# Seven-product blocks of a decoder trunk: another order of the halves, results given out one per half, standard units placed by a count of VectorE's work

## The chip, the core and the metric

The kernel runs on one core of one Trainium2 chip. The metric is the device time of one execution in microseconds (us): 1917.76 us before, the median of three runs (1916.74 to 1919.27).

## The reference

Two layers of a decoder trunk over 256 tokens of width 2048, all in float32:

```python
for l in range(DEPTH):
    h = rms_norm(x, norm1_g[l])
    z = h @ w_in[l]
    ...
    x = x + mixed @ w_out[l]
    h2 = rms_norm(x, norm2_g[l])
    x = x + (jax.nn.silu(h2 @ w_gate[l]) * (h2 @ w_up[l])) @ w_down[l]
```

What is left out is a gated spatial unit and a sliding-window attention that make `mixed`. The change touches only the last line, the feed-forward stage: gate and up projections (2048 to 5632 columns each), SwiGLU, and the down projection back to 2048.

## The kernel before

**Float32 from two parts.** A weight tile of 128 x 1024 numbers is loaded into a buffer `raw` (eight of them). ScalarE casts it to a rounded high part `wh` (`split2`, L127; five buffers), VectorE subtracts that from `raw` and gives the low part `wl` (L128; four buffers). TensorE then makes three matmuls for each product, high by high, high by low, low by high (`mm3`, L163 to L165). So each tile costs ScalarE one cast and VectorE one subtraction, and neither can run further ahead of TensorE than there are buffers.

**Standard units.** `unit` uses one tile for both token blocks: twelve matmuls of 512 columns. The down projection and block 0 of gate and up are made of these, 104 a layer, in PSUM banks named `dacc`. The down projection adds onto the residual: ScalarE copies the residual into a bank (`seed`, L1211) and the sum back out (`out_of`, L1237).

**Seven-product blocks.** For the other ten blocks of 512 columns (`S_BLOCKS`), gate and up for both token blocks are taken as one 2 x 2 product of matrices in seven multiplications in place of eight. The class `Lean` holds one block. Its methods `one` to `seven` are the seven products, each in four pieces i = 0 to 3 along the inner dimension. A piece is called a half: half of a unit's matmuls, six, from one tile. This text writes 5.2 for piece 2 of product five. The operands on the weight side are:

- 1.i and 3.i load a tile with SyncE. After 1.i's split, GpSimd issues a DMA that adds another weight tile onto that buffer (`onto`, L456). 5.i splits the sum.
- In 5.i VectorE also forms t2 = that sum + the buffer of 3.i (L471, recorded as L453), and GpSimd then issues a DMA that adds onto the buffer of 3.i. 6.i splits t2, 7.i splits the buffer of 3.i.
- 2.i loads a tile, and VectorE adds it onto t2 (recorded as L453 too); 4.i splits that.

`tc.issue_after` keeps each of these sums behind the split before it.

The products collect in five PSUM banks: m0 for one and two, m4 for three, m1 for five, m3 for six (which begins as a copy of m0, L476), m2 for seven and four. Results come out in between: m0 + six is copied out of the bank (L491), c21 = m2 + that (VectorE, recorded as L453), c21 is copied back into the bank m2 by ScalarE (L495) so that 4.i can add onto it, then c12, c22 and c12 once more on VectorE. Before, these steps stand in the method `two`, behind 2.0, 2.1, 2.2 and 2.3. Then `gated` takes Silu on ScalarE (L1162) and a multiplication on VectorE (L1163), and the activation is transposed by TensorE into `ps_f` (L246), cast (L1141) and split (L1142) for the down projection.

**What sets the order.** `lean_run` sorts all halves of all ten blocks by a table: `LEAN[m][i]` is the place of half i of product m within its block, and block n starts 28 places after block n-1. `lean_run` is a generator. The loop at L1300 takes one step of it and then as many standard units as keep their count on a straight line: 5 at first, 16 left at the end, and `HALVES` = 300 steps in between (280 halves, and two empty steps per block, after 4.3 and after 6.3). Beneath this, a scheduler settles the final order on each engine, and pools give out buffers as they come free. Each engine takes its own instructions in order, GpSimd's and SyncE's DMA issues among them.

Of the kernel before, what the change touches and what calls it, by code (L numbers as in the profile page):

```python
# [12 lines left out]
F32 = mybir.dt.float32  # L13
# [3 lines left out]
ALU = mybir.AluOpType  # L17
# [3 lines left out]
P = 128  # L21
# [73 lines left out]
def trunk(ctx, tc, x, xt, w_in, w_q, w_out, w_oa, w_uh, w_gate, w_up, w_down, sgu_w, sgu_g, consts,  # L95
# [13 lines left out]
    def f(t):  # L109
        return t.bitcast(F32)  # L110
# [6 lines left out]
        return raw  # L117

    last_wl = [None]

    def split2(raw):
# [3 lines left out]
        for j in range(0, 2, step):  # L125
            src = raw[:, j : j + step, :]
            nc.scalar.copy(wh[:, j : j + step, :], src)  # L127
            last_wl[0] = nc.vector.tensor_tensor(  # L128
                wl[:, j : j + step, :], src, f(wh[:, j : j + step, :]), ALU.subtract
            )  # L130
        return wh, wl
# [5 lines left out]
    def later(delay, fn):  # L137
        pending.append((clock[0] + delay, next(serial), fn))
# [280 lines left out]
    class Lean:  # L419
        def __init__(self, src, pairs, ext, out, end=lambda sg: None):  # L420
            self.src, self.out, self.end = src, out, end
            self.bank, self.raw, self.t2, self.z = {}, {}, {}, {}

            def a_op(k, t):
                return lambda p, h: pairs[p][:, h, k, t * P : (t + 1) * P]

            def e_op(n):
                return lambda p, h: ext[p][:, h, n, :]

            self.home = {  # L430
                1: (0, a_op(0, 0)), 2: (0, a_op(1, 0)), 3: (4, e_op(3)), 4: (2, a_op(1, 1)),
                5: (1, e_op(1)), 6: (3, e_op(2)), 7: (2, e_op(0)),
            }

        def acc(self, m):
            if m not in self.bank:
                self.bank[m] = pa.tile([P, NB], F32, tag="acc", name=f"m{m}")
            return self.bank[m]

        def half(self, n, raw, i):  # L440
            m, op = self.home[n]
            wh, wl = split2(raw)
            first, last = n in (1, 3, 5, 7) and i == 0, i == 3
            for j in range(2):
                ah, al = (op(2 * i + j, h) for h in range(2))
                mm3(
                    self.acc(m), ah, al, wh[:, j, :], wl[:, j, :], first and j == 0,
                    last and j == 1, m in (0, 2, 3),
                )
            tick(0.5)  # L450

        def add(self, out, x, y):
            nc.vector.tensor_tensor(out, x, y, ALU.add)  # L453

        def onto(self, dst, i):
            anchor[0] = nc.gpsimd.dma_start(dst, self.src(0, 1, i), accum_op=ALU.add)  # L456
# [10 lines left out]
        def five(self, i):  # L467
            self.half(5, self.raw[1, i], i)
            self.t2[i] = ap.tile([P, 2, NB], F32, tag="spt", name="t2", bufs=4)
            with tc.issue_after(last_wl[0].ins):  # L470
                self.add(self.t2[i], self.raw[1, i], self.raw[3, i])  # L471
            self.onto(self.raw[3, i], i)

        def six(self, i):
# [7 lines left out]
        def two(self, i):  # L482
            b21 = raw_load(self.src(1, 0, i))
            self.half(2, b21, i)
            with tc.issue_after(last_wl[0].ins):
                self.add(self.t2[i], self.t2[i], b21)
            z, bank = self.z, self.bank
            if i == 0:
                for v in ("m0", "c12", "c21", "c22"):
                    z[v] = zp.tile([P, NB], F32, tag="z", name=v)  # L490
                nc.scalar.copy(z["m0"], bank[3])  # L491
            elif i == 1:
                self.add(z["c21"], bank[2], z["m0"])
            elif i == 2:
                nc.scalar.copy(bank[2], z["c21"])  # L495
                self.add(z["c12"], bank[1], z["m0"])
            else:
                self.add(z["c22"], bank[1], z["c21"])
                self.add(z["c12"], bank[4], z["c12"])

        def four(self, i):
            self.half(4, self.t2[i], i)
            z, bank = self.z, self.bank
            if i == 0:
                self.out(0, bank[0], z["m0"], z["c12"])
            elif i == 3:
                later(1, lambda: self.out(1, bank[2], z["c21"], z["c22"]))
                self.end([z["m0"], z["c21"]])

    def lean_run(blocks):  # L510
        steps = sorted(
            (28 * n + LEAN[m][i], n, m, i) for n in range(len(blocks)) for m in range(7) for i in range(4)
        )
        for _, n, m, i in steps:
            b = blocks[n]
            (b.one, b.two, b.three, b.four, b.five, b.six, b.seven)[m](i)
            yield
# [108 lines left out]
    for lay in range(L):  # L626
# [510 lines left out]
        def act_T(b, c, sg, pairs_f=pairs_f):  # L1137
            ps = pm.tile([P, 2, SEQ], F32, tag="sm", name="ps_f")
            transpose_pair([sg[t][:, 2 * c * P : (2 * c + 2) * P] for t in range(NTOK)], ps)
            pair = tp.tile([P, 2, 2, SEQ], F32R, tag="aT", name="aT")  # L1140
            nc.scalar.copy(pair[:, 0], ps)  # L1141
            nc.vector.tensor_tensor(pair[:, 1], ps, f(pair[:, 0]), ALU.subtract)  # L1142
            pairs_f.setdefault(b, []).append(pair)

# [15 lines left out]

        def gated(t, psum, sg, c, rstd2=rstd2, nrstd2=nrstd2):
            nc.scalar.activation(sg, psum, AF.Silu, scale=rstd2[t])  # L1162
            nc.vector.scalar_tensor_tensor(sg, c, nrstd2[t], sg, ALU.mult, ALU.mult)  # L1163

        def s_block(b, lay=lay, pairs2=pairs2, ext2=ext2, gated=gated, act_later=act_later):
# [22 lines left out]
        def gate_up(b, even=even, act_later=act_later, seeds=seeds, left=left):  # L1188
            acc = yield from even(b, w_gate)
            sg = []  # L1190
            for t in range(NTOK):
                s = zp.tile([P, NB], F32, tag="z", name="sg")
                nc.scalar.activation(s, acc[t], AF.Silu, scale=rstd2[t])
                sg.append(s)
            acc = yield from even(b, w_up)
            for t in range(NTOK):
                nc.vector.scalar_tensor_tensor(
                    sg[t], acc[t], rstd2[t], sg[t], ALU.mult, ALU.mult
                )
                later(1.5 + 0.5 * t, lambda t=t: left[0] < NFF or seeds[0](0, t))  # L1200
            act_later(b, sg)
# [95 lines left out]
        done = 0  # L1297
        while done < FF_FIRST and next(other):
            done += 1
        for k, _ in enumerate(s_stream()):  # L1300
            while done < FF_FIRST + (k + 1) * (STD_UNITS - TAIL - FF_FIRST) / HALVES and next(other, False):
                done += 1
        seven_done[0] = True
        if lay < L - 1:
# [103 lines left out]
```

## Time and profile before

| what | value |
|---|---|
| median of the runs (3) | 1917.76 us |
| the profiled execution | 1915.93 us |
| its span, first to last instruction | 1914.2 us |
| TensorE busy | 1892.9 us, 99% |
| VectorE busy | 1685.7 us, 88% |
| ScalarE busy | 1400.8 us, 73% |
| granted TensorE clock | 1.000 |

In the profile, PE is TensorE, PEld its weight loads (which run beside the matmuls), DVE is VectorE, ACT ScalarE, POOL GpSimd, SP SyncE. A row of a group names line, engine, operation, what is written and read, shapes and count, then the busy time and the mean of one in ns, then the idle time of the engine ahead of it and who ended it. In a timeline the idle time stands in brackets at the end of a row. A chain of waits is followed back from the last instruction: each row is a start, a length and what ran or was waited for. Most executions agree within 0.3%.

### The profile page before, as it was taken

Reading aid. Unit: us, or ns where it says so; the run is one execution under the profiler, and the core shown is the slowest. Engines: PE = TensorE matmul, PEld = TensorE weight load, DVE = VectorE, ACT = ScalarE, POOL = GpSimd, SP = SyncE. Lnnn points to the kernel's source line nnn. Section 1 sums busy time; section 2 is a strip of 40 time slices with the busy share of each in tenths; the row PEclk is TensorE's granted clock in tenths of the full one; section 3 lists DMA queues with packets and bytes.
Section 4 is the critical chain, followed back from the end, with each engine's and each line's share of the span. In section 5 each row is a group of like instructions: output and inputs, shape, how many; then the busy total and the mean of one; then the engine's idle time right before and its main releaser. Section 6 shows DMA issues by size and latency. Waiting matters only on the chain.

```text
span 1914.2 us, 25497 instructions
## 1 busy us (share of the span) xinstructions
PE 1892.9 (99%) x8624; PEld 1544.8 (81%) x8624; DVE 1685.7 (88%) x1834; ACT 1400.8 (73%) x1880; POOL 218.2 (11%) x224
## 2 busy tenths in 40 slices
PE   9999999999999999999999999999999999999999
PEld 7887788888878878788888778888888888787887
DVE  7988988999889988989898888989999898988993
ACT  8668776777767777777776886767877676776774
POOL 0231001110111001100002200011110111011100
PEclk9999999999999999999999999999999999999999
DMA  9973669888988889878568648699888888888873
GB/s 355 262 285 132 189 208 241 240 223 245 259 233 218 246 246 240 224 230 257 188 219 290 192 153 233 209 259 244 220 237 255 239 235 231 242 242 239 224 236 119
DMA packets 123394, 442.15 MB, mean 231 GB/s; under 512 B 13696, under 2 KB 14080, under 8 KB 123264
## 3 DMA queue, kind: packets, MB, share of 16 engines
q1 hardware_dynamic: 94320, 336.59, 49.9%
q0 software_dynamic: 28224, 102.77, 29.3%
q8 instruction: 67, 1.10, 0.2%
q10 hardware_dynamic: 720, 1.18, 0.2%
q14 instruction: 63, 0.52, 0.1%
HBM read 438.39 MB, written 2.10 MB: 230 GB/s over the span
## 4 chain that ended last, share of the span: by engine, by line
PE 89%; DVE 4%; ACT 2%; DMA 2%; issue 2%; POOL 0%; SPq 0%; DVEq 0%; POOLq 0%; ACTq 0%
PE m L164 14%; PE m L163 14%; PE m L165 14%; PE dacc L163 11%; PE dacc L164 11%; PE dacc L165 11%; PE acc L164 3%; PE acc L165 3%; PE acc L163 3%; DMA raw<-in_w_up_dram 2%; DVE wl L128 1%; PE l L163 1%; PE l L164 1%; PE l L165 1%; PE ps_f L246 1%
## 5 line engine op out<-in xcount | busy, mean ns | idle before, releaser
L127 ACT CAST wh<-raw 128x1024 fp32r<-128x1024 f32 (+1 forms) x794 | 823.0, 1051 | 344.2 <-PE dacc L165 169.5
L128 DVE TENSOR_TENSOR wl<-raw,wh 128x1024 fp32r<-128x1024 f32 (+1 forms) x794 | 951.4, 1217 | 133.3 <-ACT wh L127 45.9
L164 PE MATMUL m<-wl,ext 128*128 128x512 f32 x704 | 274.8, 390 | 3.0 <-DVE wl L128 3.0
L163 PE MATMUL m<-wh,ext 128*128 128x512 f32 x704 | 275.6, 392 | 0.0
L165 PE MATMUL m<-wh,ext 128*128 128x512 f32 x704 | 274.3, 390 | 0.0
L456 POOL DMA_DIRECT2D raw<-in_w_up_dram x160 | 138.6, 870 | 1059.9 <-DVE wl L128 490.6
L163 PE MATMUL dacc<-wh,aT 128*128 128x512 f32 x624 | 243.2, 392 | 0.0
L164 PE MATMUL dacc<-wl,aT 128*128 128x512 f32 x624 | 243.1, 390 | 0.0
L165 PE MATMUL dacc<-wh,aT 128*128 128x512 f32 x624 | 243.1, 390 | 0.0
L128 DVE TENSOR_TENSOR wl<-t,wh 128x1024 fp32r<-128x1024 f32 x176 | 212.9, 1218 | 22.5 <-ACT wh L127 11.3
L127 ACT CAST wh<-t 128x1024 fp32r<-128x1024 f32 x176 | 184.6, 1052 | 39.7 <-PE m L165 23.0
L163 PE MATMUL m<-wh,hT 128*128 128x512 f32 x528 | 206.0, 391 | 0.0
L165 PE MATMUL m<-wh,hT 128*128 128x512 f32 x528 | 205.6, 389 | 0.0
L164 PE MATMUL m<-wl,hT 128*128 128x512 f32 x528 | 205.5, 389 | 0.0
L164 PEld LDWEIGHTS m<-wl,ext 128*128 128x128 f32 x704 | 132.2, 188 | 32.3 <-DVE wl L128 5.4
L165 PEld LDWEIGHTS m<-wh,ext 128*128 128x128 f32 x704 | 132.2, 188 | 27.5
L163 PEld LDWEIGHTS m<-wh,ext 128*128 128x128 f32 x704 | 132.2, 188 | 27.0
L165 PEld LDWEIGHTS dacc<-wh,aT 128*128 128x128 f32 x624 | 117.2, 188 | 24.5
L164 PEld LDWEIGHTS dacc<-wl,aT 128*128 128x128 f32 x624 | 117.2, 188 | 24.3 <-DVE wl L128 0.2
L163 PEld LDWEIGHTS dacc<-wh,aT 128*128 128x128 f32 x624 | 117.2, 188 | 24.0
L164 PEld LDWEIGHTS m<-wl,hT 128*128 128x128 f32 x528 | 99.2, 188 | 20.7 <-DVE wl L128 0.3
L165 PEld LDWEIGHTS m<-wh,hT 128*128 128x128 f32 x528 | 99.1, 188 | 20.5
(218 smaller groups left out, 2823.2 us busy)
## 6 DMA issues: line engine op xcount, KB each, us to landing
raw<-in_w_gate_dram SPq DMA_DIRECT2D x176, 512.0 KB, 5.2
raw<-in_w_down_dram SPq DMA_DIRECT2D x176, 512.0 KB, 5.0
raw<-in_w_up_dram POOLq DMA_DIRECT2D x160, 512.0 KB, 8.3
raw<-in_w_up_dram SPq DMA_DIRECT2D x96, 512.0 KB, 5.1
raw<-in_w_in_dram SPq DMA_DIRECT2D x68, 512.0 KB, 6.6
raw<-in_w_out_dram SPq DMA_DIRECT2D x48, 512.0 KB, 4.4
raw<-in_w_q_dram SPq DMA_DIRECT2D x32, 512.0 KB, 5.9
raw<-in_w_oa_dram SPq DMA_DIRECT2D x16, 512.0 KB, 3.7
```

What stands on the lines that cost most here:

```text
L127: nc.scalar.copy(wh[:, j : j + step, :], src)
L128: last_wl[0] = nc.vector.tensor_tensor(wl[:, j : j + step, :], src, f(wh[:, j : j + step, :]), ALU.subtract)
L163: nc.tensor.matmul(acc, ah, wh, start=first, stop=False, skip_group_check=again)
L164: nc.tensor.matmul(acc, ah, wl, start=False, stop=False, skip_group_check=again)
L165: nc.tensor.matmul(acc, al, wh, start=False, stop=last, skip_group_check=again)
L246: nc.tensor.transpose(ps[:, j, t * P : (t + 1) * P], blocks[t][:, j * P : (j + 1) * P], ident)
L456: anchor[0] = nc.gpsimd.dma_start(dst, self.src(0, 1, i), accum_op=ALU.add)
```

## The change

There are three parts.

1. *The order of the halves.* `LEAN` gets other places, and a block's period is 56 places in place of 28. The two empty steps per block are gone, and `HALVES` is 280.
2. *The results.* They no longer stand in `two` and `four`, but in a list, each with the product that must be finished for it. After each half, `settle` takes at most one from the list of each open block. Ahead of 4.0 it takes as many as are needed for the bank m2.
3. *The units.* `vec` counts VectorE's work in the order of the program: 1 for a split or a sum of a tile, 0.55 or 0.6 for the smaller ones. The loop compares this count with a usual course (1.47 per half and 1.02 per unit) and moves the count of units that are due by 0.4 of the difference. This begins after 28 steps and fades out over the last 28.

```diff
-HALVES = 30 * len(S_BLOCKS)
+HALVES = 28 * len(S_BLOCKS)
+HALF_LOAD = 1.47
+UNIT_LOAD = 1.02
+EVEN = 0.4
...
 LEAN = (
-    (0, 4, 8, 12), (24, 26, 27, 29), (6, 10, 14, 18), (30, 31, 33, 37), (7, 11, 15, 19),
-    (16, 20, 22, 23), (13, 17, 21, 25),
+    (0, 9, 17, 25), (48, 52, 55, 58), (10, 18, 26, 34), (58, 60, 64, 72), (14, 22, 30, 39),
+    (28, 36, 41, 42), (28, 36, 44, 57),
 )
...
+            self.results = [
+                ({6}, self.unite), ({7}, lambda: self.add("c21", 2, "m0")),
+                (set(), lambda: nc.scalar.copy(self.bank[2], self.z["c21"])),
+                ({5}, lambda: self.add("c12", 1, "m0")), (set(), lambda: self.add("c22", 1, "c21")),
+                ({3}, lambda: self.add("c12", 4, "c12")),
+                ({2}, lambda: self.out(0, self.bank[0], self.z["m0"], self.z["c12"])),
+                ({4}, self.finish),
+            ]
...
+        def settle(self, upto=None):
+            while self.results and self.results[0][0] <= self.done:
+                self.results.pop(0)[1]()
+                if upto is None or len(self.results) <= upto:
+                    break
...
         def half(self, n, raw, i):
             m, op = self.home[n]
+            if n == 4 and i == 0:
+                self.settle(5)
...
-            (28 * n + LEAN[m][i], n, m, i) for n in range(len(blocks)) for m in range(7) for i in range(4)
+            (56 * n + LEAN[m][i], n, m, i) for n in range(len(blocks)) for m in range(7) for i in range(4)
         )
...
-            if m in (3, 5) and i == 3:
-                yield
...
+            if k == 27:
+                load[0] = usual(k)
+
+            def due():
+                ahead = load[0] - usual(k)
+                more = EVEN * ahead * min(1, (HALVES - 1 - k) / 28) if k > 27 else 0
+                return min(FF_FIRST + (k + 1) * slope + more, STD_UNITS - TAIL)
```

**VectorE, from 5.0 to 7.0 of block 7, layer 0.** Before; t2 is the sum in 5.0, raw_6008 the buffer of 3.0, which is split at the end for 7.0; the splits between are 1.2, 4.3 of the block before (t2_5756), 3.1, 5.1 and 1.3:

```order
L453 TENSOR_TENSOR t2_6050<-raw_5916,raw_6008 128x1024
L128 TENSOR_TENSOR wl_6056<-raw_6053,wh_6055 128x1024
L128 TENSOR_TENSOR wl_6067<-t2_5756,wh_6066 128x1024
L128 TENSOR_TENSOR wl_6079<-raw_6076,wh_6078 128x1024
L128 TENSOR_TENSOR wl_6089<-raw_5985,wh_6088 128x1024
L453 TENSOR_TENSOR t2_6103<-raw_5985,raw_6076 128x1024
L128 TENSOR_TENSOR wl_6109<-raw_6106,wh_6108 128x1024
L128 TENSOR_TENSOR wl_6123<-raw_6008,wh_6122 128x1024
```

The same place on VectorE after the change, from the split of 1.2 on (the sum t2_6032 of 5.0 and the split of 4.3 stand right ahead of it); raw_6058 and raw_6138 are standard units, wl_6171 is 6.0, the last row is 7.0:

```order
L137 TENSOR_TENSOR wl_6048<-raw_6045,wh_6047 128x1024
L137 TENSOR_TENSOR wl_6061<-raw_6058,wh_6060 128x1024
L137 TENSOR_TENSOR wl_6081<-raw_6078,wh_6080 128x1024
L137 TENSOR_TENSOR wl_6099<-raw_5995,wh_6098 128x1024
L1191 SCALAR_TENSOR_TENSOR c21_5791<-c22_5792,nr_2723,c21_5791 128x512
L511 TENSOR_TENSOR t2_6108<-raw_5995,raw_6078 128x1024
L137 TENSOR_TENSOR wl_6114<-raw_6111,wh_6113 128x1024
L137 TENSOR_TENSOR wl_6141<-raw_6138,wh_6140 128x1024
L137 TENSOR_TENSOR wl_6159<-raw_6156,wh_6158 128x1024
L1169 TENSOR_TENSOR aT_6095<-ps_f_6090,aT_6095 128x512
L137 TENSOR_TENSOR wl_6171<-t2_6032,wh_6170 128x1024
L137 TENSOR_TENSOR wl_6181<-raw_6008,wh_6180 128x1024
```

Between the sum and the split of 7.0 stood five splits and one sum; now there are nine splits (two of them units), one sum and two smaller steps.

**ScalarE, the copy of c21 into the bank m2, block 6, layer 0.** Before; the casts are a unit, 1.0 of the next block, 2.3 and 4.0 (t2_5516), then the copy, then 4.1 (t2_5616):

```order
L127 CAST wh_5900<-raw_5898 128x1024
L127 CAST wh_5918<-raw_5916 128x1024
L127 CAST wh_5932<-raw_5930 128x1024
L127 CAST wh_5945<-t2_5516 128x1024
L495 COPY m2_5636<-c21_5856 128x512
L127 CAST wh_5957<-t2_5616 128x1024
```

The same place on ScalarE after the change; the casts are 2.3, (a copy of the residual into a bank,) 4.0, a unit, 4.1, 4.2 and a second unit:

```order
L136 CAST wh_5912<-raw_5910 128x1024
L1240 COPY dacc1_5879<-xres_111 128x512
L136 CAST wh_5925<-t2_5516 128x1024
L136 CAST wh_5938<-raw_5936 128x1024
L136 CAST wh_5954<-t2_5592 128x1024
L136 CAST wh_5965<-t2_5685 128x1024
L136 CAST wh_5979<-raw_5977 128x1024
L447 COPY m2_5668<-c21_5791 128x512
```

The copy stood right behind the cast of 4.0; now the casts of 4.1, 4.2 and two units are ahead of it.

**TensorE, the start of 4.0 at the same place.** Before, 4.0 follows 2.3 (m0):

```order
L164 MATMUL m0_5388<-wl_5933,hT_2806 128x512
L165 MATMUL m0_5388<-wh_5932,hT_2806 128x512
L163 MATMUL m2_5636<-wh_5945,hT_2359 128x512
L164 MATMUL m2_5636<-wl_5946,hT_2359 128x512
L165 MATMUL m2_5636<-wh_5945,hT_2359 128x512
```

After the change, a standard unit (dacc) stands between 2.3 and 4.0, and 4.0 begins ahead of that unit's last four matmuls:

```order
L172 MATMUL dacc0_5876<-wh_5938,aT_4592 128x512
L173 MATMUL dacc0_5876<-wl_5939,aT_4592 128x512
L172 MATMUL m2_5668<-wh_5925,hT_2359 128x512
L173 MATMUL m2_5668<-wl_5926,hT_2359 128x512
L174 MATMUL m2_5668<-wh_5925,hT_2359 128x512
L172 MATMUL m2_5668<-wh_5925,hT_2393 128x512
L173 MATMUL m2_5668<-wl_5926,hT_2393 128x512
L174 MATMUL m2_5668<-wh_5925,hT_2393 128x512
L174 MATMUL dacc0_5876<-wh_5938,aT_4592 128x512
```

Between the last matmul of 7.3, which c21 needs, and the first of 4.0 stood 2.1, 2.2, a unit, 1.0 of the next block and 2.3, 36 matmuls; now there are 2.3 and eight matmuls of the unit, 14.

More of the change, by code (lines that the diff above doesn't have):

```diff
@@ L438, in acc, with unite, add, finish @@
             return self.bank[m]
+        def unite(self):
+            for v in ("m0", "c12", "c21", "c22"):
+                self.z[v] = zp.tile([P, NB], F32, tag="z", name=v)
+            nc.scalar.copy(self.z["m0"], self.bank[3])
+        def add(self, out, bank, z):
+            vec(0.55)
+            nc.vector.tensor_tensor(self.z[out], self.bank[bank], self.z[z], ALU.add)
+        def finish(self):
+            later(1, lambda: self.out(1, self.bank[2], self.z["c21"], self.z["c22"]))
+            self.end([self.z["m0"], self.z["c21"]])
+        def settle(self, upto=None):
[3 more added lines that the diff above has]
+                    break
         def half(self, n, raw, i):
             m, op = self.home[n]
+            if n == 4 and i == 0:
+                self.settle(5)
             wh, wl = split2(raw)
@@ L449, in half @@
                 )
+            if last:
+                self.done.add(n)
             tick(0.5)
-        def add(self, out, x, y):
-            nc.vector.tensor_tensor(out, x, y, ALU.add)
         def onto(self, dst, i):
@@ L485, in two @@
             with tc.issue_after(last_wl[0].ins):
[L486 to L499, printed above, removed]
+                vec(1)
+                nc.vector.tensor_tensor(self.t2[i], self.t2[i], b21, ALU.add)
         def four(self, i):
             self.half(4, self.t2[i], i)
[L503 to L508, printed above, removed]
     def lean_run(blocks):
         steps = sorted(
-            (28 * n + LEAN[m][i], n, m, i) for n in range(len(blocks)) for m in range(7) for i in range(4)
+            (56 * n + LEAN[m][i], n, m, i) for n in range(len(blocks)) for m in range(7) for i in range(4)
         )
+        open_blocks = []
         for _, n, m, i in steps:
             b = blocks[n]
+            if m == 0 and i == 0:
+                open_blocks.append(b)
             (b.one, b.two, b.three, b.four, b.five, b.six, b.seven)[m](i)
+            for o in open_blocks:
+                o.settle()
+            open_blocks = [o for o in open_blocks if o.results]
             yield
-            if m in (3, 5) and i == 3:
-                yield
     def seven_low(src, pairs, ext, done, tag="hT"):
@@ L1299, in trunk, with usual @@
             done += 1
-        for k, _ in enumerate(s_stream()):
-            while done < FF_FIRST + (k + 1) * (STD_UNITS - TAIL - FF_FIRST) / HALVES and next(other, False):
+        load[0] = 0.0
+        begun = done
+        slope = (STD_UNITS - TAIL - FF_FIRST) / HALVES
+        def usual(k):
+            halves, units = k + 1, done - begun
+            return halves * HALF_LOAD + units * UNIT_LOAD
+        for k, _ in enumerate(s_stream()):
+            if k == 27:
[4 more added lines that the diff above has]
+                return min(FF_FIRST + (k + 1) * slope + more, STD_UNITS - TAIL)
+            while done < due() and next(other, False):
                 done += 1
```

12 lines of the change are left out of this document (11 added, 1 removed).

## The prediction

> **What bounds the kernel now.** I read the page first, then the waits, then the feed-forward stage in equal stretches, then the chain of waits inside one bad stretch. The engine line of the page, and one row of the waits:
>
> ```profile
> PE 1892.9 (99%) x8624; PEld 1544.8 (81%) x8624; DVE 1685.7 (88%) x1834; ACT 1400.8 (73%) x1880; POOL 218.2 (11%) x224
> ```
> ```profile
> ACT wh L127 <- DMA raw<-in_w_up_dram: 37.0, 27, 3.5
> ```
>
> TensorE has work for 99% of the span, so no reordering can win more than its gaps. The second row names something that recurs: ScalarE waits 27 times for an accumulating DMA. Now one clean stretch of the feed-forward stage, and the six with TensorE gaps (three in each layer; the columns are length, busy time of each engine with its instructions, clock, DMA share, GB/s):
>
> ```profile
> 345.00:440.00 95.00, 95.00 (x432) 78.60 (x431) 88.89 (x85) 72.28 (x87) 12.13 (x14) 1.00 0.88 239
> 535.00:630.00 95.00, 93.23 (x419) 76.83 (x418) 84.90 (x80) 68.48 (x78) 12.10 (x14) 1.00 0.87 234
> 630.00:725.00 95.00, 93.53 (x415) 76.63 (x415) 84.81 (x81) 67.89 (x77) 8.66 (x10) 1.00 0.85 237
> 725.00:820.00 95.00, 92.99 (x417) 76.22 (x416) 83.90 (x79) 67.28 (x78) 12.13 (x14) 1.00 0.88 242
> 1485.00:1580.00 95.00, 93.99 (x423) 77.53 (x422) 85.69 (x81) 69.66 (x79) 12.12 (x14) 1.00 0.87 236
> 1580.00:1675.00 95.00, 93.39 (x414) 76.39 (x413) 84.61 (x80) 66.91 (x77) 8.66 (x10) 1.00 0.84 236
> 1675.00:1770.00 95.00, 93.02 (x417) 76.17 (x415) 83.77 (x79) 68.02 (x78) 12.12 (x14) 1.00 0.87 241
> ```
>
> The gaps are 1.77 + 1.47 + 2.01 = 5.25 us in the first layer and 1.01 + 1.61 + 1.98 = 4.60 in the second: **9.85 us in all**, and nothing in this stage beside them. The clock is full everywhere. VectorE is busy 84 to 86 of 95 us where TensorE waits and 88.9 where it doesn't: it isn't short of time on average, it is late at moments. The chain of waits in the second stretch shows which:
>
> ```profile
> 667.08 1.15 DVE t L453
> 668.26 0.48 issue
> 668.75 7.84 DMA raw<-in_w_up_dram
> 676.68 1.06 ACT wh L127
> 677.77 1.14 DVE wl L128
> ...
> 684.09 0.49 ACT aT L1141
> 684.60 0.70 DVE aT L1142
> 685.35 0.65 PE ps_f L246 x4
> ```
>
> This is half 5.0 of block 7: VectorE's sum t2, then GpSimd's accumulating DMA into the same buffer, then ScalarE's cast of that buffer for half 7.0. ScalarE had stood idle for it, and its queue is then late for everything behind, down to the activation's transpose that TensorE waits for. The third stretch has the same chain:
>
> ```profile
> 794.20 9.72 DMA raw<-in_w_up_dram
> ...
> 804.34 0.79 DVE wl L128
> ...
> 808.97 0.67 DVE aT L1142
> ```
>
> So the bound is TensorE, and its gaps come from accumulating DMAs that land after their turn.
>
> **The change, part by part.** Unit prices first: a half of six matmuls, and ScalarE's and VectorE's pieces.
>
> ```profile
> 575.11 0.39 PE L163 MATMUL m<-wh,ext 128*128 128x512 f32 x1
> ...
> 575.56 0.39 PE L165 MATMUL m<-wh,ext 128*128 128x512 f32 x1
> ...
> 576.03 1.05 ACT L127 CAST wh<-t 128x1024 fp32r<-128x1024 f32 x1 [0.35 <-PE m L165]
> ...
> 576.47 0.39 PE L163 MATMUL m<-wh,ext 128*128 128x512 f32 x1
> ```
> ```profile
> L127 ACT CAST wh<-raw 128x1024 fp32r<-128x1024 f32 (+1 forms) x794 | 823.0, 1051 | 344.2 <-PE dacc L165 169.5
> L128 DVE TENSOR_TENSOR wl<-raw,wh 128x1024 fp32r<-128x1024 f32 (+1 forms) x794 | 951.4, 1217 | 133.3 <-ACT wh L127 45.9
> ```
> ```profile
> L495 ACT COPY m<-c x20: 576/588/592, 339.2 to 1852.6; 128x512 f32<-128x512 f32 x20
> ```
> ```profile
> L453 DVE TENSOR_TENSOR c<-m,m x40: 673/681/684, 338.4 to 1851.6; 128x512 f32<-128x512 f32 x40
> ```
> ```profile
> L456 POOL DMA_DIRECT2D raw<-in_w_up_dram x160: 857/863/1158, 285.3 to 1832.7; - x160
> ...
> DMA to landing us min/median/max: 5.1/8.3/11.6
> ```
>
> From 575.11 to 576.47 six matmuls start: 0.227 us each, 1.36 a half, 2.72 a standard unit. From the last start of a half (575.56) to the cast that waited for its buffer (576.03) are 0.47 us.
>
> *The order of the halves.* From VectorE's sum to the split of 7.i there is 0.5 to the issue (the "issue" row), a median of 8.3 to the landing, 1.05 for the cast and 1.22 for the split: 11.1 us. Counting matmuls in the built order at 0.227, TensorE had in layer 0, between its start of 5.i and its start of 7.i, as little as 8.2 us in blocks 7 and 9 and 10.9 in blocks 5 and 6, else 11.8 and more. Blocks 5, 7 and 9 are just the three stretches with gaps. Now the least is 15.0, and 17.3 in the place of the two 8.2. 15.0 exceeds 11.1 even if VectorE had no lead at all, so these gaps go: **up to -9.85 us**. What is late next is the other accumulation, from 1.i to 5.i, with the same 11.1: it had 10.0 at the least after block 1 (blocks 7 and 9) and has 11.4 now in seven blocks a layer and 10.9 in one, all at 1.1. It stays inside, by 0.3 and VectorE's lead (rival B).
>
> *No empty steps, fewer halves per unit.* The built programs have equally many instructions on every engine, and GpSimd's stand in the same order. This only moves things: 0.
>
> *Results one per half.* The adds, copies and Silus are the same in number. But c21, the first result, is made later: 7.3 now stands after 2.2 and the next block's 1.0, and 4.0 adds onto the bank that c21 is copied to. TensorE had 36 matmuls, 8.2 us, between 7.3 and 4.0 in most blocks. It has 14 now, 3.18 us, in six blocks of each layer (18, 4.09 us, in the four others). Queued ahead of the copy on ScalarE are the casts for 4.1, 4.2 and a second unit; the last needs the buffer of half 2.3. Counted from the last start of 7.3: 1.36 to the last start of 2.3, 0.47 to the cast, 1.05 for it, 0.59 for the copy: 3.47. TensorE wants the bank 15 starts after, at 3.41. On VectorE the sum c21 stands behind the split of 4.1, which waits for a buffer of 7.3: 0.47 + 1.22 + 0.68 = 2.37, earlier than the 2.89 at which the copy can begin. So TensorE waits about 0.1 us in 12 blocks: **+1.2 us**; from 0 (the cast and the copy overlap, as neighbours on ScalarE do) to 0.7 each, 8.4, if one more copy of 0.59 stands ahead. The nearest row is the first.
>
> *Units by the running count.* It shifts single units by a half or two. In the built order the densest places for VectorE (2.0, 2.1, 2.2, each with a sum) now have a unit between them; a unit costs TensorE 2.72 and VectorE 1.22. I take 0 for it: in these stretches VectorE has some 10 of 95 us free, and that is its cover; without it a split that comes late costs up to 1.22 a place.
>
> *Sum.* -9.85 + 1.2 = **-8.65 us**. The profiled execution took 1915.93 (its span is 1914.2, with 1.7 around it), so 1907.3; the median of the runs is 1.83 above it, and from that 1917.76 - 8.65 = **1909.1**.
>
> The Trainium skill (page "Perfetto Trace Analysis", section "Identifying the Most-Contended Engine") holds that matmul busy time is a poor measure and that the busy share of weight loads is the good one. By that rule the six stretches lack (78.60 less their second columns) 11.8 us of loading, which at the clean stretch's 78.60 of 95 is an estimated 14.3 us of work, and the time would be 1904.7. The rows here differ in how many short transposes they hold (x414 to x432), so the sum stays with the gaps.
>
> **Rivals.** *A, the copy becomes the new wait (0.12).* The order gives 4.0 only 3.41 us for a chain of 3.47. With a copy of 0.59 more ahead, each of 12 blocks waits 0.6 us: 7.2 given back, **1915.1**. For it: the residual's handover copies sit in that ScalarE queue in some blocks. Against: they stand ahead of casts that have to wait anyway.
>
> *B, slower: 1.1 to 5.1 (0.09).* Eight blocks a layer now have at most 11.4 us there. In the trace, 1.1's DMA goes out alone, 5.7 us ahead of the next:
>
> ```profile
> 663.07 0.86 POOL L456 DMA_DIRECT2D raw<-in_w_up_dram  x1 [7.90 <-DVE wl L128]
> 668.75 1.76 POOL L456 DMA_DIRECT2D raw<-in_w_up_dram  x2 [4.81 <-DVE t L453]
> ```
>
> Now the next follows two splits and a sum later, some 3.7 us. If crowding stretches its landing to the longest seen, 11.6, it needs 14.4; with a lead of one half (1.36) TensorE is 1.64 late at 16 places, 26 us: 1917.76 - 9.85 + 26 = **1934**. It turns into a loss when landings there pass 10.6. Against: 5.1 is the shortest seen, and for most of its transfer it would still be alone. The Trainium skill (page "SBUF — State Buffer", section "SBUF: two separate sides") says that DMAs issued from GpSimd have their descriptors written by its cores, which VectorE can lock out of a shared port; a VectorE with fewer pauses would then stretch the landings. The trace speaks against it: of 160 issues the median is 863 ns and the longest 1158, with VectorE busy nine tenths of the time.
>
> *C, it doesn't do it (0.09).* The landings are late for want of DMA bandwidth (share 0.84 to 0.88 in all seven stretches) and move with the order; then the gaps stay where TensorE meets them: **1917.8**. Against: the clean stretch has the same 0.88.
>
> **How the numbers follow.** The forecast, fewer gaps and a copy just in time, gets 0.70: 1909.1, by itself from 1906.9 (all gaps gone, nothing added, 1 us for the runs' spread) to 1912 (0.35 us at each 4.0). A reaches 1915.1. The range **1906.5 to 1915.5** holds both, 0.82, and leaves B and C out. A measurement of this kernel tells about 0.2%, 3.8 us, from no change. Below 1913.9 lie the forecast and the milder part of A: faster 0.75; the rest of A and C: same 0.16; B: slower 0.09.
>
> **What would show it.** Right: the same stretches show 94.5 us and more of TensorE; ScalarE's 27 waits for the accumulating DMA shrink to a few short ones; TensorE's only new wait is for the copy into m2, near 0.1 us. Wrong: a TensorE wait of over 0.5 us per block ahead of 4.0 (A), ScalarE waits for the DMA at 5.1 in every block (B), or gaps of the old size with landings over 11 us (C).

## The result, and the profile after

After the change the kernel takes **1906.84 us** (median of 6 runs, 1904.58 to 1907.8), beside 1917.89 us of the kernel before in the same session (6 runs, 1916.74 to 1919.75). The ratio is 0.9939, with a 95% interval of 0.9926 to 0.9952; on the 1917.76 us of the earlier runs that is 1906.1. The forecast was 1909.1, with a range from 1906.5: the sign and the kind of cause are the forecast ones, and the gain is some 2.3 to 3 us larger.

These are the stretches of the feed-forward stage again, in the profile after (length, busy time of TensorE, its weight loads, VectorE, ScalarE and GpSimd with their instructions, clock, DMA share, GB/s):

```profile
535.00:630.00 95.00, 95.00 (x428) 78.27 (x427) 86.92 (x82) 70.47 (x81) 12.11 (x14) 1.00 0.87 235
630.00:725.00 95.00, 95.00 (x424) 78.33 (x423) 87.96 (x83) 70.11 (x79) 9.55 (x11) 1.00 0.87 247
725.00:820.00 95.00, 95.00 (x428) 78.67 (x427) 86.75 (x80) 70.12 (x80) 12.13 (x14) 1.00 0.90 240
...
1675.00:1770.00 95.00, 95.00 (x428) 78.66 (x427) 85.83 (x80) 70.78 (x81) 10.40 (x12) 1.00 0.91 245
```

TensorE is busy for all 95 us of each, and it holds some ten matmuls more in each stretch than before. The accumulating DMA as the profile after groups it (who waited for it, in us and times, and the time from issue to landing):

```profile
  ACT wh L136: 2.9, 5
...
DMA to landing us min/median/max: 5.3/8.7/11.5
```

ScalarE's 37.0 us in 27 waits are now 2.9 us in 5. The landings are no shorter than before (median 8.7 against 8.3); the turns come later.

The one new wait is the forecast one, ahead of 4.0. In block 6 of layer 0, first ScalarE's queue (the casts of 4.1, 4.2 and a unit, then the copy of c21 into m2):

```profile
592.82 1.06 ACT L136 CAST wh<-t 128x1024 fp32r<-128x1024 f32 x1 [1.03 <-PE dacc L174]
594.18 1.06 ACT L136 CAST wh<-t 128x1024 fp32r<-128x1024 f32 x1 [0.30 <-PE m L174]
595.54 1.06 ACT L136 CAST wh<-raw 128x1024 fp32r<-128x1024 f32 x1 [0.30 <-PE m L174]
596.49 0.59 ACT L447 COPY m<-c 128x512 f32<-128x512 f32 x1
```

Then TensorE's matmuls around the start of 4.0, and the line of the copy over the whole kernel:

```profile
596.92 0.39 PE L173 MATMUL dacc<-wl,aT 128*128 128x512 f32 x1
597.15 0.48 PE L172 MATMUL m<-wh,hT 128*128 128x512 f32 x1
597.47 0.39 PE L173 MATMUL m<-wl,hT 128*128 128x512 f32 x1
```
```profile
  PEld m L172: 2.9, 12
```

The copy ends at 597.08, the weights of 4.0 follow, and the step from 597.15 to 597.47 is 0.32 us where 0.227 is the pace: 0.09 us lost. There are 12 such places. The 2.9 us of that row are the weight loader's waits, 0.24 each, most of which its lead covers.

**Stage by stage.** Both kernels have the same 8624 matmuls, so a stage can be measured between the same two of them: from the last normalization transpose ahead of the feed-forward stage to the last transpose into ps_f. Before it takes 634.60 us in layer 0 and 633.45 in layer 1, after it 628.57 and 628.16: **-11.3 us** together. What lies between the two stretches, the attention of layer 1 above all, takes 315.0 us before and 315.1 after. All the change is in the feed-forward stage.

### The profile page after: what moved, and what is told of

Its sections match the earlier page's. It is cut to its first block, busy times and chain, and to the rows that moved or that the text cites. A ratio compares the mean times of both kernels' runs of the same rounds, so it can differ in the third digit from the quotient of the medians.

```text
span 1904.8 us, 25485 instructions
## 1 busy us (share of the span) xinstructions
PE 1893.6 (99%) x8624; PEld 1546.5 (81%) x8624; DVE 1686.3 (89%) x1834; ACT 1404.8 (74%) x1880; POOL 218.6 (11%) x224
## 4 chain that ended last, share of the span: by engine, by line
PE 93%; DVE 3%; ACT 1%; issue 1%; DMA 1%; POOL 0%; SPq 0%; DVEq 0%; ACTq 0%; POOLq 0%
PE m L172 15%; PE m L173 15%; PE m L174 15%; PE dacc L172 11%; PE dacc L173 11%; PE dacc L174 11%; PE acc L173 4%; PE acc L172 4%; PE acc L174 3%; PE l L172 1%; PE l L173 1%; PE l L174 1%; DVE wl L137 1%; PE ps_f L255 1%; PE ps_n L255 1%
## 5 line engine op out<-in xcount | busy, mean ns | idle before, releaser
L172 PEld LDWEIGHTS m<-wh,hT 128*128 128x128 f32 x528 | 99.1, 188 | 22.7 <-ACT m L447 2.9
L174 PEld LDWEIGHTS m<-wh,hT 128*128 128x128 f32 x528 | 99.1, 188 | 20.8
```

The costliest lines, as they stand in the source:

```text
L172: nc.tensor.matmul(acc, ah, wh, start=first, stop=False, skip_group_check=again)
L174: nc.tensor.matmul(acc, al, wh, start=False, stop=last, skip_group_check=again)
```

## The experiments

The table sums up the profiled runs. Blocks are counted from 1 in each layer; there are 20 in all. The second and third columns are ScalarE's waits in us and times, as the profile puts them down: for an accumulating DMA, with the pieces at which most of that time falls, and for a plain load by SyncE (counted between 285 and 1830 us). The fourth is the feed-forward stage of both layers, measured as above, the last the median time of the runs.

| kernel | for the accumulating DMA | for a plain load | stage | time |
|---|---|---|---|---|
| before | 37.0, 27 (7.0, 5.2, 7.2) | 1.7, 1 | 1268.1 | 1917.9 |
| after | 2.9, 5 (7.2) | 0 | 1256.7 | 1906.8 |
| e2 units on a straight line | 2.3, 2 (5.1) | 22.5, 9 | 1259.5 | 1907.9 |
| e3 old order | 49.5, 33 (7.3, 7.0) | 0 | 1269.9 | 1916.5 |
| e4 results at once | 3.7, 6 (7.2) | 0 | 1255.5 | 1904.7 |
| e5 before, sevens later | 49.7, 20 (5.2) | 6.8, 5 | 1290.0 | 1936.2 |
| e6 after, sevens sooner | 352.8, 56 (7.2, 7.1, 7.0) | 0 | 1524.9 | 2172.0 |
| e7 after, last seven sooner | 11.2, 17 (7.3, 7.2) | 0 | 1255.4 | 1904.5 |
| e8 old order, sevens later | 25.5, 21 (5.2) | 0.2, 1 | 1265.6 | 1916.6 |
| e9 old order, sevens and fives later | 0.7, 1 | 0.6, 1 | 1255.7 | 1904.0 |
| e10 before, half transfers | 2.0, 2 (7.0) | 0 | 1255.9 | 1904.7 |
| e11 before, sevens and fives later | 22.7, 15 (7.3) | 19.5, 9 | 1271.2 | 1921.1 |
| e12 e4 and e7 together | 9.4, 16 (7.3, 7.2) | 0 | 1257.3 | 1906.7 |

My theory: the gaps are those of accumulating DMAs that land after their turn, and the new order alone takes them away. The rivals: the count of VectorE's work or the spread results do it (VectorE is late at moments), or the gaps would move with any order.

### Is the gap the DMA's? (e1, e10)

*e1* is the kernel before, unchanged, for the size of chance.

> The kernel before, unchanged, timed against itself. If the profile of before was an ordinary execution, the profile of this run shows again some 9.9 us of TensorE gaps in the three stretches of each layer, and the ratio is 1.000. If instead the gaps vary from run to run, because the landings of the accumulating DMAs do (the medians moved by 11.0 us, the two profiles by only 9.1), this profile shows gaps of 11 to 13 us and a time near 1918.

It took 1916.47 us, ratio 1.000 (0.9989 to 1.0011), and its profile shows 12 gaps again, 11.6 us from start to start of the matmuls (11.8 before); ScalarE waits 33.7 us, 27 times, for the accumulating DMA.

*e10* leaves order, results and units as before and makes the DMA shorter. It leaves out half of the addition onto each tile.

```diff
-            anchor[0] = nc.gpsimd.dma_start(dst, self.src(0, 1, i), accum_op=ALU.add)
+            anchor[0] = nc.gpsimd.dma_start(dst[:, 0:1, :], self.src(0, 1, i)[:, 0:1, :], accum_op=ALU.add)
```

> The kernel before, with GpSimd's accumulating DMAs adding only the first 512 of the 1024 columns of each tile (half of the addition is left out, the count of DMAs stays). If the gaps come from the landings of these DMAs, these get some us shorter, ScalarE's waits for them all but go and with them the gaps: 1906.5 us (1905 to 1909). If VectorE's queue in that order makes the gaps and the DMA only happens to be last: 1914 to 1918.

The line of the accumulating DMA in this run:

```profile
  ACT wh L127: 2.0, 2
...
DMA to landing us min/median/max: 3.6/5.8/8.4
```

The landings are 2.5 us sooner in the median, all but two of the waits are gone, and with them all gaps but one of 0.4 us: 1904.67 us, ratio 0.9929 (0.9916 to 0.9941). VectorE's and ScalarE's queues and the places of the halves are those of before. So the late landing is the cause, and no queue by itself. (The edit also moves 42 MB less, of 442; that less traffic elsewhere helps isn't excluded by this run alone, but *e9* below has all the traffic, landings as late as before, and no gap above 0.2 us.)

### Which part of the change does it? (e2, e3, e4)

*e2* is the changed kernel without the running count.

```diff
-EVEN = 0.4
+EVEN = 0.0
```

> The changed kernel with the running count switched off (its weight 0): new order of halves and new results, units on the straight line. By the theory (a gap comes where an accumulating DMA has less than some 11 us of TensorE work to land in) nearly all of the gain stays, 1907 to 1911: all distances from 5 to 7 are still 15.0 us and more, but one distance from 1.1 to 5.1 falls to 8.2 us in each layer and one wait for the copy into m2 has 2.04 us in place of 3.18, so 1 to 2 us come back in each layer, at these two places. By the rival (VectorE's bunched work makes the gaps, and the count spreads it) most of the gain goes: 1913 to 1917, with gaps in most blocks.

1907.9 us, ratio 0.9960 (0.9947 to 0.9974), and the feed-forward stage is 2.8 us longer than after. The time is as expected, and so is the piece. One of ScalarE's waits is at 5.1 of block 7, in its timeline; the two rows behind it are TensorE's waits that follow:

```profile
671.63 1.05 ACT L136 CAST wh<-raw 128x1024 fp32r<-128x1024 f32 x1 [2.03 <-DMA raw<-in_w_up_dram]
```
```profile
677.20 0.50 PE L173 MATMUL m<-wl,hT 128*128 128x512 f32 x1 [0.76 <-DVE wl L137]
682.34 0.33 PE L255 MATMUL ps_f<-ident,m 128*128 128x128 f32 x1 [0.52 <-DVE aT L1169]
```

This run has three gaps above 0.15 us on TensorE, 2.28 us from start to start. Followed back, all three end at this wait and at its counterpart in block 7 of layer 1. Only the block differs from the expected one: block 9 has the shortest distance (8.2 us in matmuls, 6.8 on VectorE), but its 1.1 lands after 5.2 and 5.4 us; in block 7 it takes 8.3 and 7.4. The count keeps such short distances away: after the change VectorE has 8.7 us and more from the split of 1.1 to that of 5.1 in every block.

A second thing shows in the line of SyncE's plain loads:

```profile
  ACT wh L136: 22.5, 9
```

After the change no cast waits for a plain load. With units on the straight line nine do, 2.5 us each (five units and four pieces 3.3), though the order of the halves is the same. No gap above 0.15 us goes back to any of them: here TensorE's lead covers them. The loads are late because the eight buffers `raw` are taken: seven of the nine were issued right as VectorE finished with a buffer. A tile that is split twice is held from the start of its first split to the end of its second for 16.2 us on average before, 18.9 after and 19.6 here: the new order pays for its longer distances with buffers.

*e3* is the changed kernel with the old table, doubled to the period of 56.

```diff
-    (0, 9, 17, 25), (48, 52, 55, 58), (10, 18, 26, 34), (58, 60, 64, 72), (14, 22, 30, 39),
-    (28, 36, 41, 42), (28, 36, 44, 57),
+    (0, 8, 16, 24), (48, 52, 54, 58), (12, 20, 28, 36), (60, 62, 66, 74), (14, 22, 30, 38),
+    (32, 40, 44, 46), (26, 34, 42, 50),
```

> The changed kernel with the halves in the old order (old places doubled, period 56, no empty steps), results one per half and units by the count as changed. The built order has no distance from 5 to 7 under 10.9 us now (8.2 before), 10.9 in most blocks at 5.3 to 7.3, and none from 1 to 5 under 12.3. By the theory the two 8.2 us gaps of each layer are gone, and 10.9 costs between nothing and 1.8 us (before it had one gap and one place without): 1908 to 1914. If the order of the halves in itself made the gain: 1916 to 1918. If the count alone made it: 1907, with no gap at all.

1916.47 us, ratio 1.000 (0.9991 to 1.001): a miss. I had expected the count and the spread results to bring part of the gain. They bring nothing without the order:

```profile
  ACT wh L136: 49.5, 33
```

The waits are even more. Counting casts that begin within 0.1 us of their landing after ScalarE stood idle for over 0.15, they are at 7.3 in 16 of 20 blocks and at 7.0 in 13. (Such counts are higher than the profile's row where a wait is put down to another engine.) The gaps are only spread: 24 of 0.2 to 1.2 us, 10.8 in all, instead of 12 larger ones.

*e4* is the changed kernel with all results given out as soon as their product is finished.

```diff
-                if upto is None or len(self.results) <= upto:
+                if upto is not None and len(self.results) <= upto:
```

> The changed kernel with all results that are ready taken at once after a half, not one per half. Distances of the DMAs are those of the changed kernel, and the copy into m2 has 4.09 us in place of 3.18 in six blocks of a layer. By the theory, giving the results out one per half brings nothing: 1906 to 1908, and the waits of 0.1 us ahead of 4.0 are gone. By the rival, in which VectorE's bunched sums hold up its splits, there are new TensorE gaps of 0.5 us and more per block behind the results: 1912 and more.

1904.66 us, ratio 0.9947 (0.9934 to 0.9959), and the stage is 1.2 us shorter than after: the waits ahead of 4.0 are gone. One per half brings nothing, and costs what was forecast for it.

### How long must the turns be apart? (e5, e8, e11, e9, e6)

The prediction held 11.1 us to be the need of every accumulation. By that, moving the sevens alone should be enough. *e5* does so in the kernel before:

```diff
-    (16, 20, 22, 23), (13, 17, 21, 25),
+    (16, 20, 22, 23), (16.5, 20.5, 23.5, 25),
```

> The kernel before, with one part of its table of places changed: 7.0, 7.1 and 7.2 stand three halves later (7.3 stays). From 5 to 7 there are 15.0 us and more then, in place of 8.2; from 1 to 5 the least falls from 10.0 to 8.6, in blocks 7 and 9. Results in two and four, straight line and empty steps as before. The TensorE gaps of the feed-forward stages were 11.8 us before and 0.2 after the change. By the theory (gaps come from accumulating DMAs with too little TensorE work to land in) this alone takes 8 to 11 us of them, with what is left in blocks 7 and 9: 1907 to 1910. By the rival (it takes the new order as a whole, the results and the count) it brings at most 2 us.

1936.19 us, ratio 1.0095 (1.0074 to 1.0116): slower, the plainest miss. 7.i used to stand between 1.2 and 5.2. Without it TensorE has, counted in matmuls as in the prediction, 8.6 us from 1.2 to 5.2 in blocks 7 and 9, 11.4 in 5 and 6, and 14.6 in most others; and by the same count the cast of 5.2 waits in 17 of 20 blocks. GpSimd's issues in block 7 (two in the row, 3.0 and 1.2), then ScalarE's queue, then the matmuls that waited:

```profile
681.24 1.76 POOL L456 DMA_DIRECT2D raw<-in_w_up_dram  x2 [4.81 <-DVE t L453]
```
```profile
687.24 0.68 ACT L1162 ACTIVATE c<-m,ir 128x512 f32<-128x512 f32 x1
692.49 1.05 ACT L127 CAST wh<-raw 128x1024 fp32r<-128x1024 f32 x1 [4.57 <-DMA raw<-in_w_up_dram]
```
```profile
693.59 0.50 PE L163 MATMUL m<-wh,ext 128*128 128x512 f32 x1 [0.74 <-ACT wh L127]
694.85 0.50 PE L164 MATMUL m<-wl,ext 128*128 128x512 f32 x1 [0.76 <-DVE wl L128]
697.12 0.50 PE L164 MATMUL m<-wl,ext 128*128 128x512 f32 x1 [0.62 <-DVE wl L128]
699.10 0.33 PE L246 MATMUL ps_f<-ident,m 128*128 128x128 f32 x1 [0.55 <-DVE aT L1142]
```

1.2's DMA goes out right behind that of 3.0, at 682.1, and lands 10.3 us later; ScalarE stands idle for 4.57 us, and four gaps follow. This is the general picture. Sorted by piece, the median landing before was 6.5 us for 1.0, **5.4 for 1.1**, 8.2 for 3.0, **10.6 for 1.2**, 8.3 for 3.1, **10.3 for 1.3**, 8.5 for 3.2 and 7.9 for 3.3. 1.2 and 1.3 are the ones that are issued right behind another; 1.1 goes out alone. The need isn't one number: from VectorE's split of 1.2 to its split of 5.2 it is 0.3 to the issue, 10.3 and more to the landing and 1.2 to the cast's end and the split's start, 11.8 us.

*e8* does the same in e3, to see the old order without its short way to 7.i:

```diff
-    (32, 40, 44, 46), (26, 34, 42, 50),
+    (32, 40, 44, 46), (33, 41, 47, 50),
```

> The kernel with the old order, the new results and the count, which came out no faster than before, with its sevens later (7.0 to 7.2 as in the run on the kernel before). From 5 to 7 there are 12.3 us at the least (5.3 to 7.3, five blocks a layer) in place of 10.9 in eleven places a layer. By the theory what it lost goes with the distances: 1907 to 1910, feed-forward stages of 1256 to 1260 us in place of 1269.9. If something else in the old order holds it up, it stays at 1914 and more.

1916.56 us, ratio 0.9992 (0.9982 to 1.0003): a miss of the same kind. The waits at 7.0 to 7.2 are gone; some are left at 7.3, and 11 of 20 blocks wait at 5.2 instead, though most have 14.6 us of matmuls since 1.2. All of TensorE's gaps above 0.2 us (9.3 us) go back to 5.2:

```profile
  ACT wh L136: 25.5, 21
```

*e11* moves 5.2 and 5.3 as well, in the kernel before:

```diff
-    (0, 4, 8, 12), (24, 26, 27, 29), (6, 10, 14, 18), (30, 31, 33, 37), (7, 11, 15, 19),
-    (16, 20, 22, 23), (13, 17, 21, 25),
+    (0, 4, 8, 12), (24, 26, 27, 29), (6, 10, 14, 18), (30, 31, 33, 37), (7, 11, 16.75, 20.75),
+    (16, 20, 22, 23), (16.5, 20.5, 25, 25.5),
```

> The kernel before with eight numbers of its table changed: 5.2, 5.3 and the sevens later, all else (results, units, empty steps) as before. 1.2 to 5.2 has 16.4 us and more, 1.3 to 5.3 16.4 and more, but 7.3 comes only 9.5 us after 5.3 in three blocks of ten, and 7.0 11.4 after 5.0 in two. If the pieces' own needs decide (7.i about 11): waits for the DMA at 7.3 in those three blocks alone, gaps of some 1.5 us each there, 1910 us (1907 to 1913). If moving the sevens costs by itself, as when they alone were moved (1936): 1925 or more.

1921.11 us, ratio 1.002 (1.0011 to 1.003). (The edit changes six numbers, not eight.) No wait at 5.2 or 5.3 is left, as expected, but 14 of 20 blocks wait at 7.3, and not the three with 9.5 us alone: the 12.3 us of matmuls in the others aren't enough either. The two lines (accumulating DMA, then plain loads) show a second cause beside it:

```profile
  ACT wh L127: 22.7, 15
```
```profile
  ACT wh L127: 19.5, 9
```

One of the nine: SyncE had no free buffer from 676 to 681, and ScalarE's cast came 3.86 us late.

```profile
675.89 0.33 SPq L116 DMA_DIRECT2D raw<-in_w_down_dram  x1
681.05 0.33 SPq L116 DMA_DIRECT2D raw<-in_w_up_dram  x1
```
```profile
688.18 1.05 ACT L127 CAST wh<-raw 128x1024 fp32r<-128x1024 f32 x1 [3.86 <-DMA raw<-in_w_up_dram]
```

This wait leads to no gap by itself. The tiles are held 18.9 us here, as after the change, but the units stand on the straight line, as in e2. Followed back to their last wait, of the 13.7 us of gaps above 0.15 us 10.0 go to 7.3's DMA and 3.6 to two plain loads, in block 9 of each layer.

*e9* is e3 with the sevens, 5.2 and 5.3 later, and 7.3 far enough behind 5.3:

```diff
-    (60, 62, 66, 74), (14, 22, 30, 38), (32, 40, 44, 46), (26, 34, 42, 50),
+    (60, 62, 66, 74), (14, 22, 33.5, 41.5), (32, 40, 44, 46), (33, 41, 50.5, 54.5),
```

> The changed kernel with the old order's table, but with the sevens and also 5.2 and 5.3 later. Between its start of 1.2 and of 5.2 TensorE then has 14.6 us and more, for 1.3 to 5.3 13.6 and more, for 5.i to 7.i 14.1 and more, for 1.1 to 5.1 12.3 and more. If each piece has a need of its own (1.2 and 1.3 about 13.3 us, 7.i about 11, 1.1 about 8.2), no gap is left and no copy waits: 1905.5 us (1904 to 1908). If the old order costs by something else than these distances (it took 1916.5 with and without later sevens): 1913 to 1917.

**1904.02 us**, ratio 0.9924 (0.9912 to 0.9937). One wait of 0.7 us is left, and no gap above 0.15 us in layer 0:

```profile
  ACT wh L136: 0.7, 1
...
DMA to landing us min/median/max: 5.2/8.6/11.7
```

The landings are as late as ever (1.2's take 10.4 us in the median). Six numbers of a table make the stage 14.2 us shorter than in e3, and give the old order what the new one has. The tiles are held for 19.1 us; with the count of VectorE's work, only one plain load is late.

*e6* goes the other way, with the first three sevens sooner than after:

```diff
-    (28, 36, 41, 42), (28, 36, 44, 57),
+    (28, 36, 41, 42), (20, 28.5, 37, 57),
```

> The changed kernel with 7.0, 7.1 and 7.2 five to seven places sooner, so that from 5 to 7 there are 6.8 to 8.6 us in three of four halves of every block, in place of 15.0 to 20.5; from 1 to 5 nothing gets shorter, results and count as changed. By the theory the gaps come back, and in every block, not in three: at 8.2 us a place cost 1.6 us and more before, so 20 blocks cost 30 us or more: 1930 to 1950. By the rival (VectorE's bunched work) the time stays at 1907 to 1910.

2171.95 us, ratio 1.1321 (1.1294 to 1.1348), where I had expected a tenth of that loss (by the table, the three sevens stand seven to eight places sooner):

```profile
  ACT wh L136: 352.8, 56
```

That is 6.3 us a wait. A wait isn't paid once: with ScalarE late, the next accumulations go out late as well (3.1's was issued 10.3 us after its split in the median, where after the change it is 3.7). A part of the loss is something else, the clock of TensorE:

```profile
core 0: 2171.9 us, clock 0.962
```

In the other profiles the granted clock is 0.998 to 1.000. Here it is at half in 35 stretches, 168.8 us in all, and the matmuls of the feed-forward stage that start in them lose some 72 us against their usual step, of the 268 us by which the stage is longer than after the change. Whether the waits brought the clock down isn't shown by a run of its own; of the other kernels, one stretch of 3.4 us at half clock falls into the feed-forward stage of e5, right behind a gap of 2.5 us.

So TensorE's matmuls are the wrong clock to count on. VectorE runs ahead of TensorE by more or less, and less where 1.2 is split than where 5.2 is. These are the times on VectorE in the profiles (the least and the median of 20 blocks in us, a wait included where there was one): from the end of 1.2's split to the start of 5.2's, and from the issue of the DMA onto 3.0's and 3.3's buffers to the splits of 7.0 and 7.3:

| | before | after | e5 | e8 | e11 | e9 |
|---|---|---|---|---|---|---|
| 1.2 to 5.2 | 10.0, 13.5 | 12.5, 14.9 | 10.3, 12.2 | 9.9, 11.9 | 13.0, 15.4 | 13.6, 15.4 |
| 3.0 to 7.0 | 8.5, 10.0 | 12.8, 14.4 | 16.7, 19.1 | 17.5, 18.6 | 9.1, 14.2 | 11.3, 14.1 |
| 3.3 to 7.3 | 10.4, 11.5 | 14.3, 15.5 | 10.2, 13.4 | 10.0, 11.6 | 8.1, 9.4 | 12.0, 12.3 |

The need is some 11.8 us in the first row, and a landing of 7.8 to 9.1 and 1.2, so 9 to 10.3, in the others. In the four kernels of the table with long waits (before, e5, e8 and e11) most of the waiting is at the row whose median stands nearest to its need, and only after and e9 are clear of it in all three. A place that isn't in the table is tight after the change: 3.2 to 7.2, with 10.2 us at the least and 10.9 in the median. Four of its five short waits are there, too short for TensorE to notice.

### Can the copy's wait go too? (e7, e12)

*e7* is the changed kernel with 7.3 three places sooner, so that 4.0 comes 5.5 us and more after it.

```diff
-    (28, 36, 41, 42), (28, 36, 44, 57),
+    (28, 36, 41, 42), (28, 36, 44, 54),
```

> The changed kernel with 7.3 three places sooner, ahead of 2.2: between it and 4.0 TensorE has 5.5 to 9.5 us then, in place of 3.2 to 4.1; from 5.3 to 7.3 13.6 us in place of 16.4 to 19.1. By the prediction's working, the wait for the copy into m2 (0.1 us in 12 blocks) goes, and nothing else changes: 1.1 us, the feed-forward stages 1255.6 us in place of 1256.7. If 13.6 us is too little for the DMA, gaps show at 7.3 in every block, and it is 1910 and more.

1904.48 us, ratio 0.9929 (0.991 to 0.9947), the stage 1.3 us shorter than after. ScalarE now has 17 waits of 0.66 us for the DMA, 11.2 in all, and TensorE doesn't notice: so short a wait is inside its lead.

*e12* joins e4 and e7.

> The changed kernel with the last seven at 54 and all results given out as soon as they can be. Each edit alone gave 1904.5 to 1904.7. If both remove the same wait, the copy ahead of 4.0, the two together give no more than one: 1904.5 (1903.5 to 1905.5). If they remove different ones: 1902.5.

1906.72 us, ratio 0.9939 (0.9925 to 0.9952). The two don't add, as they remove the same wait; the stage is 1.9 us longer than in e7, which the expectation didn't have. TensorE's weight loads show the larger part of it, a wait that neither e4 nor e7 has:

```profile
PEld dacc L172 <- ACT dacc L1240: 3.3, 12, 0.3
```

Twelve units wait for the copy of the residual into their bank, 0.11 us each from start to start, 1.3 us. What the two edits together do to bring these copies so late wasn't followed. e4, e7 and e9 are some 2 us faster than the change itself in their medians, with intervals that overlap with its own; by the stage, 1.0 to 1.3 us shorter, they are the better versions by a little, if at all.

## Why the prediction was right and wrong, step by step

**The bound and its cause: right.** TensorE's gaps come from accumulating DMAs that land after their turn. e10 shows it with the order left alone, e9 with the landings left alone.

**"Blocks 5, 7 and 9 are just the three stretches": wrong for block 5.** The prediction put all gaps to the distance from 5 to 7. Followed back, 8.5 of the 11.8 us before (blocks 7 and 9) go to the cast of 7.0, but 3.3 (block 5, and a small one in block 8) to that of 5.2, the other accumulation. This is its wait in block 5 of layer 0, ahead of the first gap of the second stretch:

```profile
555.28 1.05 ACT L127 CAST wh<-raw 128x1024 fp32r<-128x1024 f32 x1 [1.84 <-DMA raw<-in_w_up_dram]
```

1.2's DMA had gone out at 543.8 and landed at 555.2, after 11.4 us; 7.0's had landed at 550.3, and its cast didn't wait. The new order gives 5.2 more room as well (12.7 us of matmuls in block 5, then 15.8), so these gaps went too; but the prediction didn't forecast it, and that part of the gain is luck.

**"9.85 us in all": the step that failed.** That the gaps go was right, their size wasn't. I read the gaps as what TensorE's busy time lacks in a stretch. These are two of its rows before, at the first gap of the second stretch:

```profile
559.49 0.39 PE L165 MATMUL m<-wh,ext 128*128 128x512 f32 x1
561.65 0.33 PE L246 MATMUL ps_f<-ident,m 128*128 128x128 f32 x1 [1.77 <-DVE aT L1142]
```

From start to start are 2.16 us, and a matmul in step takes 0.227: the gap is 1.93 us. The record of a matmul runs for 0.39, 0.16 longer than its step, and covers the beginning of each gap, so that the busy time lacks only 1.77. Before there are 12 gaps above 0.15 us, and from start to start they come to 11.83 us; after there is one of 0.15. So the term was -11.7 and not -9.85, and about 2 of the 2.3 to 3 us that the forecast was off are this. The steps that are longer than usual by 0.02 to 0.15 us add up to 4.8 us before and 5.4 after, the copy's 12 places (1.1 us) among them: -11.7 + 0.6 = -11.1, where the stage measured -11.3 and the medians -11.05.

The Trainium skill (page "Perfetto Trace Analysis", section "Identifying the Most-Contended Engine") warns against matmul busy time as a measure. The trace agrees with the warning (0.16 us hidden in each gap). The busy share of weight loads, one of the two measures that it gives instead, led to 14.3 us, more than the 11.7 to be had: the true term lies between the two.

**"11.1 us": the same for all pieces: wrong.** It was a median landing, and landings differ by piece: 5.4 us for 1.1, over 10 for 1.2 and 1.3. And it was set against TensorE's matmuls, where VectorE's lead changes from the one place to the other. The change was still judged rightly, since it gives the pieces that waited longest enough (12.5 us on VectorE for 5.2 at the least, 12.8 for 7.0), and 7.2 and 5.1 so nearly enough that TensorE loses nothing. But by the rule e8, with 10.9 us and more everywhere after block 1 and 14.6 from 1.2 to 5.2 in most blocks, should have won nearly all, and it won nothing that can be measured.

**"Late next", 1.1 to 5.1: right in place, and it held.** The tightest of the fives after the change is 5.1: in block 2 of layer 1 its cast waits 0.6 us, without a gap on TensorE, and in the other blocks it begins 0.6 us after the landing at the least. Without the count it is the one that waits (e2). The landing there is 5.5 us in the median and 7.6 at most. Rival B's turning point wasn't near; by the prediction's own terms it is 10.0 (11.6 less the 1.64), not 10.6. The longer landings behind another DMA, which B rested on, exist, but at 1.2 and 1.3, which have room.

**The copy, +1.2 us: right.** 12 places of 0.09 us; without them the stage is 1.2 (e4) or 1.3 us (e7) shorter. Rival A's further copy doesn't stand in the way.

**The running count, 0: wrong.** It is worth 2.8 us of the stage (e2), of which 2.3 are gaps behind 5.1 in block 7. VectorE's free time, which I named as the cover, isn't what this turns on: where the units stand decides how long the distance from 1.1 to 5.1 is. The 11.4 us that the prediction worked with there already contain the count; without it the distance falls to 10.9 in blocks 5 and 7 and to 8.2 in block 9. So the gain is not the order's alone.

**Results one per half, nothing besides the copy: right** (e4). **Rival C: wrong.** The DMA share stays at 0.87 to 0.91, the landings stay late, and the gaps go.

**The range.** Its lower end was "all gaps gone, nothing added", worked out with the 9.85. With 11.8 it would have been 1904.9, and e9 and e7 come out at or just below that end: 1904.0 and 1904.5. The 1906.1 of the result lies just under the stated 1906.5.

## What to carry to other kernels

Measure a TensorE gap from start to start of its matmuls less their step, not by missing busy time. For a DMA that adds onto a buffer in use, count the time between the two turns for each piece by itself, with the landing that this piece shows in the trace: here one issued right behind another took twice as long as one issued alone. And when such a distance is lengthened, look at both neighbours: the distance that it shortens (e5), and the loads that wait for the buffers now held longer (e11). And look through a wait of ScalarE to TensorE before counting it as lost: e2 has 22.5 us of them that cost no gap.

## What the runs showed of the hardware beyond that

**Landing by company.** The same DMA of 512 KB from GpSimd lands after 5.4 us when it goes out alone (1.1), and after 10.3 to 10.6 behind another (1.2, 1.3). With half the bytes these are 3.7, 6.0 and 6.8 us. By the shortest landings of all, 5.1 and 3.6 us, 256 KB cost 1.5 us; on a straight line through these two, an estimate, some 2 us would not depend on the size.

**The start isn't the same in every run.** TensorE's work ahead of the feed-forward stage is the same in all kernels. But the last normalization transpose ahead of it starts at 287.2 us before, at 290.2 in e1, which is the same kernel, and at up to 291.4 (e4). A part of the difference is there from the first loads on. One and the same matmul, before and in e7 (290.8):

```profile
14.21 0.50 PE L164 MATMUL acc<-wl,hT 128*128 128x512 f32 x1 [0.17 <-DVE wl L128]
```
```profile
16.32 0.50 PE L173 MATMUL acc<-wl,hT 128*128 128x512 f32 x1 [0.47 <-DVE wl L137]
```

So two profiled spans can differ by 3 us where the change has no part in it, as much as the forecast was off: the spans of before and after (1914.2 and 1904.8) differ by 9.4 us, the stage that was changed by 11.3.
